# Rotating an 8192 x 8192 matrix by 90 degrees: the last two stores issued in three and four pieces

## The chip, the cores and the metric

The kernel runs on one core of a Trainium2 chip. The metric is the device time of one execution in microseconds (us), the median of several. A core has engines that run side by side (PE multiplies and transposes, DVE and ACT copy, POOL and SP do little here) and 16 DMA engines that move data between the memory (HBM) and the core's on-chip buffer (SBUF), which has 128 partitions. Transfers are issued by SP (here the loads) and by ACT (here the stores); each issuer has its own queue, and both queues are served by the same 16 DMA engines.

## The reference

```python
def setup_inputs():
    return {
        "x": np.random.randn(8192, 8192).astype(np.float32),
        "k": 1,
    }

def reference(x: np.ndarray, k: int) -> np.ndarray:
    return np.rot90(x, k)
```

With k = 1, row i of the output is column 8191 - i of the input: a transpose, and the order of the rows reversed. 268.4 MB are read and 268.4 MB are written; nothing else is computed.

## The kernel before

The input is cut into 16 macro tiles of 1024 rows by 4096 columns. A macro tile is loaded in T = 8 loads of 128 rows (128 partitions of 16 KB, 2 MB each), 128 loads in all. DVE copies each loaded tile into a ring of slots, with the columns reversed (L202). PE transposes blocks of 128 x 128 from the ring into two halves of PSUM (`ps0`, `ps1`, L234). ACT copies each half from PSUM into a store buffer (L265, two copies for each store) and then issues the store (L270), 128 stores of 2 MB in all.

Five buffers of 16 KB for each partition serve all transfers: two for landing loads (`LAND`) and three for stores (`OUTS`); for the first macro tile all five take loads, and for the last eight stores all five take stores. A load waits until DVE has read the buffer's last load; the first copy of a store waits until the last store from its buffer has landed, which is counted in `s_store[b]`, 16 for each transfer.

A store of the first 15 macro tiles writes 512 output rows of 1024 columns. Those of the last macro tile write 1024 output rows of 512 columns (`END` = 4 tiles of rows, two groups of columns): for each of the 128 partitions eight pieces of 2 KB, one in each of eight output rows that lie 128 rows apart. On the SBUF side a partition is one run of 16 KB; `whole_reads` writes it that way into the instruction.

The order of the work is written out by hand, one program for each engine. ACT's program is the loop over the stores: wait for the buffer, copy, copy, wait for both copies (`s_ev`), issue the store, go on to the next. SP's program issues the loads and then, at the end, waits for the last store of every buffer (L188), after which the closing barrier runs. After the last load has landed, only stores remain in the queues; the last eight stores are counted by n = 120 to 127, and the last two of them are n = 126 and n = 127. No later store uses their buffers.

Of the kernel before, what the change touches and what calls it, by code (L numbers as in the profile page):

```python
# [6 lines left out]
P = 128  # L7
# [10 lines left out]
CH = G * P  # L18
# [5 lines left out]
H = 2  # L24
LAND = 2
OUTS = 3


def whole_reads(nc):
# [17 lines left out]
def slot(kk, t, j):  # L47

    at = t * J + j if kk % 2 == 0 else J + t + j * T
    return (at + kk // 2 * (J + 1)) % SLOTS  # L50


def kernel(tc: tile.TileContext, x: bass.AP, k: bass.AP, out: bass.AP):
# [8 lines left out]
    n_out = KK * J  # L62
# [18 lines left out]
    with tc.tile_critical():  # L81
        ident = nc.alloc_sbuf_tensor("ident", [P, P], dt)
        scratch = nc.alloc_sbuf_tensor("scratch", [P, 1], dt)
        bufs = [nc.alloc_sbuf_tensor(f"buf{i}", [P, F], dt) for i in range(LAND + OUTS)]
        ring = nc.alloc_sbuf_tensor("ring", [P, SLOTS * CH], dt)
# [5 lines left out]
        s_id = nc.alloc_semaphore("s_id")  # L91
        s_land = [nc.alloc_semaphore(f"s_land{i}") for i in range(LAND + OUTS)]
        s_store = [nc.alloc_semaphore(f"s_store{i}") for i in range(LAND + OUTS)]
        s_rev = nc.alloc_semaphore("s_rev")
# [4 lines left out]
        def load_buf(m):  # L99
            return m % (LAND + OUTS) if m < T else m % LAND  # L100

        def out_buf(n):
            e = n - (n_out - J)
            if e < 0:
                return LAND + (n + 1) % OUTS
            ends = [load_buf(n_load - 2)]
            ends += [LAND + (n_out - J + i + 1) % OUTS for i in range(OUTS)]
            ends += [load_buf(n_load - 1)]
            return ends[e % len(ends)]
# [25 lines left out]
        def runs(kk, t, lo, hi):  # L135

            at = [slot(kk, t, j) for j in range(lo, hi)]
            i = 0
            while i < len(at):
                n = 1  # L140
                step = at[i + 1] - at[i] if i + 1 < len(at) else 1
                if step > 0:
                    while i + n < len(at) and at[i + n] - at[i + n - 1] == step:
                        n += 1
                else:
                    step = 1
                yield lo + i, n, at[i], step
                i += n

        def load(e, m):  # L150
            r0, c0 = macros[m // T]
            b = load_buf(m)
            e.dma_start(  # L153
                out=bufs[b][:], in_=x[r0 + m % T * P : r0 + (m % T + 1) * P, c0 : c0 + W]
            ).then_inc(s_land[b], 16)

        def uses_before(n_or_m, buf):
            return sum(buf(i) == buf(n_or_m) for i in range(n_or_m))

        for m in range(LAND + OUTS):  # L160
            load(nc.sync, m)
# [1 line left out]
        with nc.Block() as block:  # L163

            @block.gpsimd
            def _(e):
                e.memset(ident[:], 0.0).then_inc(s_id, 1)  # L167
                e.wait_ge(s_id, 1)
                e.affine_select(  # L169
                    out=ident[:],  # L170
                    in_=ident[:],
                    compare_op=mybir.AluOpType.not_equal,
                    fill=1.0,
                    base=0,
                    pattern=[[-1, P]],
                    channel_multiplier=1,
                ).then_inc(s_id, 1)

            @block.sync
            def _(e):  # L180
                for m in range(LAND + OUTS, n_load):
                    last = [i for i in range(m) if load_buf(i) == load_buf(m)]
                    e.wait_ge(s_rev, rev[last[-1], J - 1])
                    load(e, m)
                for b in range(LAND + OUTS):
                    n = sum(out_buf(i) == b for i in range(n_out))
                    if n:
                        e.wait_ge(s_store[b], 16 * n)  # L188

            @block.vector  # L190
            def _(e):
                for m in range(n_load):
                    kk, t = divmod(m, T)
                    b = load_buf(m)
                    a = bufs[b][:].rearrange("p (j c) -> p j c", c=CH)
                    e.wait_ge(s_land[b], 16 * (uses_before(m, load_buf) + 1))
                    for lo, hi, wait in pieces[m]:
                        if wait:
                            e.wait_ge(*wait)
                        for j, n, at, step in runs(kk, t, lo, hi):  # L200
                            v = ring[:, at * CH : (at + (n - 1) * step + 1) * CH]
                            i = e.tensor_copy(  # L202
                                out=bass.AP(
                                    tensor=v.tensor,
                                    offset=v.offset,
                                    ap=[v.ap[0], [step * CH, n], [1, CH]],
                                ),
                                in_=a[:, j : j + n, ::-1],
                            )
                        i.then_inc(s_rev, 1)  # L210

            @block.tensor
            def _(e):
                seen = {}

                def wait(sem, n):
                    if seen.get(sem, 0) < n:
                        seen[sem] = n
                        e.wait_ge(sem, n)

                e.wait_ge(s_id, 2)
                for n, (kk, ts, js) in enumerate(outs):
                    blocks = [(j, g) for j in reversed(js) for g in range(G)]
                    half = len(blocks) // H
                    rows = len(ts) * P

                    def transpose(t, b):
                        j, g = blocks[b]
                        if n:
                            wait(s_ev, H * (n - 1) + b // half + 1)  # L230
                        wait(s_rev, rev[kk * T + t, j])
                        at = slot(kk, t, j) * CH + g * P
                        f = b % half * rows + (t - ts[0]) * P
                        i = e.transpose(  # L234
                            ps[b // half][:, f : f + P], ring[:, at : at + P], ident[:]
                        )
                        if t == ts[-1] and b % half == half - 1:
                            i.then_inc(s_half, 1)
                        elif t == ts[0] and b == len(blocks) - 1:
                            i.then_inc(s_first, 1)  # L240

                    order = [(t, b) for b in range(len(blocks)) for t in ts]
                    if js[0] == 0:
                        order.sort()
                    for t, b in order:
                        transpose(t, b)

            @block.scalar
            def _(e):
                e.wait_ge(s_id, 2)  # L250
                e.copy(scratch[:], ident[:, :1])  # L251
                for n, (kk, ts, js) in enumerate(outs):
                    r0, c0 = macros[kk]
                    rows = len(ts) * P
                    b = out_buf(n)
                    for h in range(H):
                        if h == 0:
                            stores = uses_before(n, out_buf)
                            loads = [i for i in range(n_load) if load_buf(i) == b]
                            if stores:  # L260
                                e.wait_ge(s_store[b], 16 * stores)
                            elif loads:
                                e.wait_ge(s_rev, rev[loads[-1], J - 1])
                        e.wait_ge(s_half, H * n + h + 1)  # L264
                        e.copy(  # L265
                            bufs[b][:, h * F // H : (h + 1) * F // H], ps[h][:]
                        ).then_inc(s_ev, 1)
                    top = M - c0 - (js[-1] + 1) * CH
                    e.wait_ge(s_ev, H * (n + 1))
                    e.dma_start(  # L270
                        out=out[
                            top : top + len(js) * CH, r0 + ts[0] * P : r0 + ts[0] * P + rows
                        ].rearrange("(g m) f -> m g f", m=P),
                        in_=bufs[b][:].rearrange("m (g f) -> m g f", f=rows),
                    ).then_inc(s_store[b], 16)


# [33 lines left out]
```

## Time and profile before

| What | Value |
|---|---|
| time, median of 3 runs | 1266.09 us (1265.68 to 1266.21) |
| time of the profiled execution | 1266.16 us |
| its span, first to last instruction | 1264.2 us |
| PE, DVE, ACT busy | 715.5, 402.9, 467.6 us |
| DMA moved | 537.48 MB, mean 425 GB/s |
| loads (q1), stores (q10) | 268.44 MB each |
| issue of a store on ACT | 0.547 us (median of 128) |
| wait of SP for the last stores (L188) | 63.3 us in two waits |

The time of the profiled execution is 2.0 us longer than its span: that is what lies around the instructions. The page gives busy time by engine and by slice of the span; a DMA share of 1.00 means that all 16 DMA engines are moving a packet. A packet is what one DMA engine moves at a time; the trace lists each with its start, duration, size and queue, but not with the number of its DMA engine. Engine after engine works through its packets with no gap, so a packet's predecessor on the same engine is the one that ends where it starts.

### The profile page before, as it was taken

What the parts mean: (1) busy time and instruction counts of PE and PEld (TensorE: products, weight loads), DVE (VectorE), ACT (ScalarE), POOL (GpSimd) and SP (SyncE); (2) the same over time, 40 slices, a digit from 0 to 9 for tenths busy, and PEclk for the clock granted to TensorE, in tenths of its full rate; (3) what the DMA queues carried; (4) which work ended last, traced back from release to release, by engine and by line L of the source; (5) the groups of instructions that cost most, each with busy time, mean ns of one, the idle gap of its engine ahead of it and who ended that gap; (6) DMA issues with size and microseconds to landing.
All of it is one profiled execution on the core that took longest, in us unless ns stands there. A gap on an engine that the chain in (4) does not pass through costs nothing.

```text
span 1264.2 us, 9359 instructions
## 1 busy us (share of the span) xinstructions
PE 715.5 (57%) x4096; PEld 666.9 (53%) x4096; DVE 402.9 (32%) x313; ACT 467.6 (37%) x258; POOL 0.7 (0%) x6
## 2 busy tenths in 40 slices
PE   1565555665556556665556654565555655546573
PEld 1455555655546555554545544565454654545573
DVE  3322432234322343233342333422234222443210
ACT  0433334333343332433424334243342434324354
POOL 0000000000000000000000000000000000000000
PEclk9976767667777776777777767676676776767777
DMA  9999999999999999999999999999999999999998
GB/s 397 423 429 430 429 427 429 429 430 429 428 429 429 430 430 427 427 430 430 428 430 427 429 430 429 427 427 428 429 428 428 427 430 428 428 427 426 427 425 335
DMA packets 36904, 537.48 MB, mean 425 GB/s; under 512 B 4096, under 2 KB 4096, under 8 KB 4096
## 3 DMA queue, kind: packets, MB, share of 16 engines
q10 hardware_dynamic: 18432, 268.44, 50.0%
q1 hardware_dynamic: 18432, 268.44, 49.8%
q8 instruction: 32, 0.52, 0.2%
q14 instruction: 8, 0.07, 0.0%
HBM read 268.44 MB, written 268.44 MB: 425 GB/s over the span
## 4 chain that ended last, share of the span: by engine, by line
DMA 78%; issue 10%; DVE 5%; ACT 3%; PE 2%; ACTq 0%; SPq 0%
DMA buf<-in_x_dram 77%; DVE ring L202 5%; ACT buf L265 3%; PE ps L234 2%; DMA out_dram<-buf 1%; ACTq L270 0%; SPq L153 0%; ACTq L264 0%; SPq L306 0%; SPq L81 0%
## 5 line engine op out<-in xcount | busy, mean ns | idle before, releaser
L234 PE MATMUL ps<-ident,ring 128*128 128x128 f32 x4096 | 715.5, 353 | 530.3 <-ACT buf L265 394.6
L234 PEld LDWEIGHTS ps<-ident,ring 128*128 128x128 f32 x4096 | 666.9, 188 | 578.7 <-ACT buf L265 433.6
L265 ACT COPY buf<-ps 128x2048 f32<-128x2048 f32 x256 | 466.2, 1870 | 779.6 <-DMA out_dram<-buf 502.0
L202 DVE COPY ring<-buf 128x512 f32<-128x512 f32 (+7 forms) x313 | 402.9, 1336 | 815.4 <-DMA buf<-in_x_dram 814.4
L251 ACT ACT_TABLE_LOAD x1 | 1.3, 1283 | 0.9 <-SPq L81 0.9
L169 POOL TENSOR_SCALAR_AFFINE_SELECT ident<-ident 128x128 f32<-128x128 f32 x1 | 0.3, 292 | 0.2 <-POOL ident L167 0.2
L167 POOL MEMSET ident<- 128x128 f32 x1 | 0.2, 204 | 0.5 <-SPq L81 0.5
L251 ACT COPY scratch<-ident 128x1 f32<-128x1 f32 x1 | 0.2, 191 | 0.0
L292 POOL MEMSET const-bfloat16-1.0<- 128x1 bf16 x1 | 0.1, 102 | 0.0
L292 POOL MEMSET const-uint8-127<- 128x1 uint8 x1 | 0.1, 102 | 0.0
L292 POOL MEMSET const-float32-0.0<- 128x1 f32 x1 | 0.1, 98 | 0.2 <-issue 0.2
L292 POOL MEMSET const-float32-1.0<- 128x1 f32 x1 | 0.1, 98 | 0.0
## 6 DMA issues: line engine op xcount, KB each, us to landing
buf<-in_x_dram SPq DMA_DIRECT2D x128, 2048.0 KB, 16.8
out_dram<-buf ACTq DMA_DIRECT2D x128, 2048.0 KB, 25.6
```

The costliest lines, as they stand in the source:

```text
L167: e.memset(ident[:], 0.0).then_inc(s_id, 1)
L169: e.affine_select(out=ident[:], in_=ident[:], compare_op=mybir.AluOpType.not_equal, fill=1.0, base=0, pattern=[[-1, P]], channel_multiplier=1,
L202: i = e.tensor_copy(out=bass.AP(tensor=v.tensor, offset=v.offset, ap=[v.ap[0], [step * CH, n], [1, CH]],), in_=a[:, j : j + n, ::-1],)
L234: i = e.transpose(ps[b // half][:, f : f + P], ring[:, at : at + P], ident[:])
L251: e.copy(scratch[:], ident[:, :1])
L265: e.copy(bufs[b][:, h * F // H : (h + 1) * F // H], ps[h][:]).then_inc(s_ev, 1)
L292: nc = _bacc.Bacc("TRN2", target_bir_lowering=False, num_devices=1)
```

## The change

The store loop issues the second to last store as three transfers, of partitions 0 to 111, 112 to 119 and 120 to 127, and the last as four, of partitions 0 to 111, 112 to 119, 120 to 123 and 124 to 127. All pieces of a store are issued by ACT one behind the other, after the same wait for both copies, and count into the same semaphore; what waits for it counts pieces instead of stores. The other 126 stores are issued as before, and what is written where is the same.

```diff
+PIECES = {-2: [112, 8, 8], -1: [112, 8, 4, 4]}
...
+        def loads_before(m):
+            return sum(load_buf(i) == load_buf(m) for i in range(m))
+
+        def store_pieces(n):
+            return PIECES.get(n - n_out, [P])
+
+        def stores_of(b, n):
+
+            return sum(len(store_pieces(i)) for i in range(n) if out_buf(i) == b)
...
-                    n = sum(out_buf(i) == b for i in range(n_out))
+                    n = stores_of(b, n_out)
                     if n:
                         e.wait_ge(s_store[b], 16 * n)
...
-                            stores = uses_before(n, out_buf)
+                            stores = stores_of(b, n)
...
-                    e.dma_start(
-                        out=out[
-                            top : top + len(js) * CH, r0 + ts[0] * P : r0 + ts[0] * P + rows
-                        ].rearrange("(g m) f -> m g f", m=P),
-                        in_=bufs[b][:].rearrange("m (g f) -> m g f", f=rows),
-                    ).then_inc(s_store[b], 16)
+                    dst = out[
+                        top : top + len(js) * CH, r0 + ts[0] * P : r0 + ts[0] * P + rows
+                    ].rearrange("(g m) f -> m g f", m=P)
+                    src = bufs[b][:].rearrange("m (g f) -> m g f", f=rows)
+                    p = 0
+                    for k in store_pieces(n):
+                        e.dma_start(out=dst[p : p + k], in_=src[p : p + k]).then_inc(
+                            s_store[b], 16
+                        )
+                        p += k
```

More of the change, by code (lines that the diff above doesn't have):

```diff
@@ L155, in load @@
             ).then_inc(s_land[b], 16)
-        def uses_before(n_or_m, buf):
-            return sum(buf(i) == buf(n_or_m) for i in range(n_or_m))
+        def loads_before(m):
[4 more added lines that the diff above has]
+            return sum(len(store_pieces(i)) for i in range(n) if out_buf(i) == b)
         for m in range(LAND + OUTS):
@@ L195, in _ @@
                     a = bufs[b][:].rearrange("p (j c) -> p j c", c=CH)
-                    e.wait_ge(s_land[b], 16 * (uses_before(m, load_buf) + 1))
+                    e.wait_ge(s_land[b], 16 * (loads_before(m) + 1))
                     for lo, hi, wait in pieces[m]:
```

## The prediction

> **What bounds the kernel now.** I read the page first: the busy share of the DMA engines in 40 slices, then the counts of packets and the queues.
>
> ```profile
> span 1264.2 us, 9359 instructions
> ...
> DMA  9999999999999999999999999999999999999998
> ...
> DMA packets 36904, 537.48 MB, mean 425 GB/s; under 512 B 4096, under 2 KB 4096, under 8 KB 4096
> ...
> q10 hardware_dynamic: 18432, 268.44, 50.0%
> q1 hardware_dynamic: 18432, 268.44, 49.8%
> ```
>
> The reader is to see that the DMA engines are full from the first slice to the last but one, and that no compute engine matters until then. The lines also give the size of the unit of work. The stores (q10) are 128 transfers and 18432 packets, so 144 each: 128 packets of 16 KB, one for each partition, and 16 small ones (the 4096 under 512 B are 16 for each of the 256 transfers), one as the last of each engine. So a store today gives each of the 16 engines 8 packets. The data packets of q10 take 50.0% of 16 x 1264.2 us; over 16384 packets that is 0.617 us each, 26.5 GB/s for an engine.
>
> Then the table of windows over the last 14 us. Its last three columns are granted clock, share of the 16 DMA engines, and GB/s.
>
> ```profile
> 1250.00:1255.00 5.00, 0.00 (x0) 0.00 (x0) 0.00 (x0) 0.00 (x0) 0.00 (x0) 0.50 1.00 419
> 1255.00:1257.00 2.00, 0.00 (x0) 0.00 (x0) 0.00 (x0) 0.00 (x0) 0.00 (x0) 0.50 0.82 344
> 1257.00:1258.00 1.00, 0.00 (x0) 0.00 (x0) 0.00 (x0) 0.00 (x0) 0.00 (x0) 0.50 0.67 279
> 1258.00:1259.00 1.00, 0.00 (x0) 0.00 (x0) 0.00 (x0) 0.00 (x0) 0.00 (x0) 0.50 0.35 147
> 1259.00:1260.00 1.00, 0.00 (x0) 0.00 (x0) 0.00 (x0) 0.00 (x0) 0.00 (x0) 0.50 0.24 98
> 1260.00:1261.00 1.00, 0.00 (x0) 0.00 (x0) 0.00 (x0) 0.00 (x0) 0.00 (x0) 0.50 0.08 33
> 1261.00:1262.00 1.00, 0.00 (x0) 0.00 (x0) 0.00 (x0) 0.00 (x0) 0.00 (x0) 0.50 0.04 16
> 1262.00:1264.20 2.20, 0.00 (x0) 0.00 (x0) 0.00 (x0) 0.00 (x0) 0.00 (x0) 0.50 0.00 0
> ```
>
> Times 16, the share is the number of engines still at work: all up to 1255, about 11 in 1257 to 1258, four in 1259 to 1260, one after 1260. The packet records say it sharper: seven engines send their last small packet at 1256.4 to 1256.5, eight between 1258.5 and 1260.0, and one, which I call the straggler, at 1262.2. It holds the end alone for 2.2 us. Everything behind it (the wait at L188, the closing barrier) takes the 2.0 us to 1264.2.
>
> Last, the timeline of ACT, which issues the stores.
>
> ```profile
> 1239.55 0.55 ACTq L270 DMA_DIRECT2D out_dram<-buf  x1
> ...
> 1243.87 0.55 ACTq L270 DMA_DIRECT2D out_dram<-buf  x1
> 1244.51 3.63 ACT L265 COPY buf<-ps 128x2048 f32<-128x2048 f32 x2 [0.67 <-PE ps L234]
> 1248.17 0.55 ACTq L270 DMA_DIRECT2D out_dram<-buf  x1
> ```
>
> The last two stores are issued at 1243.87 and 1248.17. The early engines finish the store before them at 1246.5 (16 packets of 0.617 ahead of 1256.4) and the second to last at 1251.5, so the queue is always ahead of them.
>
> **The change, part by part.** The edits to the counts of semaphores (L188, the wait before an eviction, the loads' count) add no instruction and no wait on an earlier store, since no other store is cut: 0.
>
> Five more issues on ACT: 0.547 us each. Two of them stand before the copies of the last store, which then begins to issue 2 x 0.59 = 1.2 us later, at 1249.35. At 1235.24 an issue found idle engines and its first packet started at 1236.44, so the data flow 1.2 us after an issue: 1250.55 here. The engines first need them after seven packets of the second to last store, at 1246.5 + 4.3 = 1250.8. So they are hidden, by 0.25 us in the tightest case. If that cover is gone, early engines idle for up to 1.2 us, which matters only if they end last. The last piece is issued by 1251.6, far before it is needed. Slow issues of 0.94 and 1.17 us occur (1222.25, 1226.95); two of these would push early engines by under 1.5 us.
>
> How the packets are dealt out: 112 partitions, dealt like 128, are 7 for each engine. A piece of 8 has eight packets; I take it that they stay whole, one for each of eight engines, always the first eight, and a piece of 4 goes to the first four (bounds: spread evenly over 16, half a packet each; or all on one engine, 4.9 us). The Trainium skill ("DMA: Bandwidth & Descriptors", section "Why a DMA increments its semaphore by 16 and not by 1") deals in the same way, to the lowest-numbered engines; no run here shows it yet. In the two stores together the first four engines then get 14 ordinary packets and 5 from small pieces (19 where they had 16), the next four 14 and 3 (17), the last eight 14.
>
> The price of a packet in a small piece is what the trace doesn't show: eight engines reading eight neighbouring partitions at once. Today each engine has 8 partitions of its own, so 26.5 GB/s may belong to the engine or to a sixteenth of the partitions; both give 425 GB/s. If to the engine, a packet costs 0.617 us, the lower bound. If to the partitions, it depends on which eight share a lane: dealt one by one over the lanes, 0.617 again; eight neighbours on one lane, 8 x 0.617 = 4.9 us, the upper bound; in between, two groups of four, 4 x 0.617 = 2.5 us. I take the middle, 2.5 us: a lane of the partitions' own explains as well as one of the engines why the engines run so evenly at 26.5 GB/s each, and of its three layouts this one lies between. A piece of 4 then also costs 2.5 us. The Trainium skill ("SBUF — State Buffer", section "Door 1: The DMA port swizzle") speaks against the change in just this way: four neighbouring partitions share one of 16 ports, and partitions 0 to 3 alone gave 27.6 GB/s. By its figures a packet of a small piece would be an estimated 2.4 us; by the engine's own row, 0.617.
>
> **The sum.** First four engines: 14 x 0.617 + 5 x 2.5 = 21.1 us where 16 x 0.617 = 9.9 stood: +11.2. Next four: 8.6 + 7.5 = 16.1: +6.2. Last eight: -1.2. The trace has no engine numbers. Seven engines that end within 0.2 us of each other look like neighbours, so I take the first four to be among them: 1256.4 + 11.2 = 1267.6, which is 5.4 later than the straggler's 1262.2. The end behind it is unchanged, so the span is 1269.6. The profiled execution took 1266.16 for a span of 1264.2, 0.07 over the median of 1266.09: **1271.6 us**. If the first four hold ordinary late engines (1260.0), it is 1275.2; if the straggler, 1277.4. With 1.9 us a packet it is 1268.6.
>
> **Rivals.** (A) *The lane belongs to the engine.* A small packet costs 0.617 like any other and only the counts matter. If the straggler is one of the last eight, it sheds two packets: 1262.2 - 1.2 = 1261.0; the early engines have room (1256.4 + 1.9 = 1258.3): **1264.9 us**. If it is of the middle four, +0.6: 1266.8; of the first four, +1.9: 1268.0. For it: no packet of the whole execution shows two engines slowing each other by a factor. Against it: no two engines ever read neighbouring partitions as the small pieces do. The Trainium skill (the DMA page again, "Latency and other measured facts") calls engines 7 and 15 usually slower; by that the straggler is one of them, which leaves 1264.9 and 1266.8. (B) *The cut of 112 itself collides*: seven partitions for each engine no longer match groups of eight, and ordinary packets slow down too. Three of the 14 ordinary packets at double price add 1.9 us to the forecast: 1273.5. For it is the same argument as for the forecast; against, that such collisions are brief. (C) *The pieces are not dealt as I think*: spread evenly over the 16 engines, every engine keeps 16 packets' worth, and the end stays: 1266.2. (D) *A real gain*, over 0.2%: from 1256.45 on, the engines do some 28 engine-us, so a perfect balance would end 4.0 us earlier, at 1262.2 us. But no engine sheds more than two packets here; only a straggler that comes from luck in its last microseconds would allow it.
>
> **How the numbers follow.** 0.2% (2.5 us) is about what a measurement of this kernel can tell from no change. Forecast with its sizes 0.46, own range 1268.7 to 1273; B and the late first four 0.14, 1273 to 1277; together 0.60 slower. A 0.32, of which 1264.9 has 0.22 (its best case has the engines in the order that the straggler needs), 1266.8 and 1268.0 0.10; C 0.03: 0.35 within. D 0.05 faster. The range reaches down to A, as it holds a third, and up into B: 1264.6 to 1273.6; some 0.15 is left out.
>
> **What would show it.** Each step has its sign in the profile of the changed kernel: 133 issues where 128 stood; q10 with 18464 packets (32 more small ones: 160 packets for each cut store) if each piece ends in one small packet for each engine that it uses; in the last 20 us packets of some 2.5 us, and a DMA share of about 0.25 (four engines) for several microseconds at the end. Packets of 0.62 us throughout and a last one near 1261.0 would make A right; an idle stretch between 1250 and 1252 would say that the later issue matters. The prediction is wrong if no packet of the small pieces takes much over 0.62 us.

## The result and the profile after

The changed kernel takes 1271.78 us (median of 4 runs, 1271.16 to 1272.32) against 1265.95 us (1265.68 to 1266.21) for the kernel before: a ratio of 1.0045, with a 95% interval of 1.0034 to 1.0057. It is 5.8 us slower. The profiled execution is the fastest of the four, 1271.16 us for a span of 1269.3 us, 5.1 us longer than before. From the page of the changed kernel:

```profile
span 1269.3 us, 9364 instructions
...
DMA  9999999999999999999999999999999999999997
...
DMA packets 36936, 537.48 MB, mean 423 GB/s; under 512 B 4128, under 2 KB 4128, under 8 KB 4128
...
q10 hardware_dynamic: 18464, 268.44, 50.1%
```

The bytes are the same, and the 32 additional packets are the small ones that close each piece on each engine that it uses: a piece of 8 uses eight engines, a piece of 4 four. Until slice 38 the row of the DMA engines is the same, and no slice's rate differs by more than 4 GB/s. The table of windows over the end of the changed kernel (last three columns: granted clock, share of the 16 DMA engines, GB/s):

```profile
1243.00:1247.00 4.00, 2.42 (x22) 2.14 (x20) 0.00 (x0) 0.40 (x1) 0.00 (x0) 1.00 1.03 414
1247.00:1250.00 3.00, 0.00 (x0) 0.00 (x0) 0.00 (x0) 0.00 (x0) 0.00 (x0) 0.57 1.03 344
1250.00:1253.00 3.00, 0.00 (x0) 0.00 (x0) 0.00 (x0) 0.99 (x1) 0.00 (x0) 0.50 1.00 328
1253.00:1255.00 2.00, 0.00 (x0) 0.00 (x0) 0.00 (x0) 2.00 (x2) 0.00 (x0) 0.50 0.42 131
1255.00:1257.00 2.00, 0.00 (x0) 0.00 (x0) 0.00 (x0) 0.65 (x1) 0.00 (x0) 0.50 0.21 82
1257.00:1262.00 5.00, 0.00 (x0) 0.00 (x0) 0.00 (x0) 0.00 (x0) 0.00 (x0) 0.50 1.01 328
1262.00:1264.00 2.00, 0.00 (x0) 0.00 (x0) 0.00 (x0) 0.00 (x0) 0.00 (x0) 0.50 0.42 156
1264.00:1266.00 2.00, 0.00 (x0) 0.00 (x0) 0.00 (x0) 0.00 (x0) 0.00 (x0) 0.50 0.23 66
1266.00:1267.50 1.50, 0.00 (x0) 0.00 (x0) 0.00 (x0) 0.00 (x0) 0.00 (x0) 0.50 0.05 22
1267.50:1269.30 1.80, 0.00 (x0) 0.00 (x0) 0.00 (x0) 0.00 (x0) 0.00 (x0) 0.50 0.00 0
```

Two things are new. From 1247 to 1253, and again from 1257 to 1262, all engines are busy, yet they move 328 to 344 GB/s where the kernel before, with all engines busy, moved 419: packets last longer. In the packet records, 83 store packets of the changed kernel that start after 1240 take over 0.75 us (the longest 3.1 us); of the kernel before, one does. And between 1253 and 1257 most engines have nothing to do. ACT's part of the chain of waits of the changed kernel (start, length, what) shows why:

```profile
1243.42 0.62 ACTq L285
1244.04 0.04 issue
1244.08 5.16 ACTq L285
1249.23 0.03 issue
1249.26 2.65 ACTq L285
```

The issue of the first small piece holds ACT for 5.16 us and that of the second for 2.65 us, where 0.547 us each was forecast. ACT can only then copy and issue the last store, as its timeline shows:

```profile
1243.42 8.49 ACTq L285 DMA_DIRECT2D out_dram<-buf  x3
1252.01 3.63 ACT L274 COPY buf<-ps 128x2048 f32<-128x2048 f32 x2 [8.62 <-issue]
1255.68 7.25 ACTq L285 DMA_DIRECT2D out_dram<-buf  x4
```

The last store is issued at 1255.68, 7.5 us later than in the profile before. So three explanations compete: slow packets, late issue, and one engine's additional packets.

### The profile page after: what moved, and what is told of

Read it like the earlier page. It is cut to its first block, busy times and chain, and to the rows that moved or that the text cites. A ratio compares the mean times of both kernels' runs of the same rounds, so it can differ in the third digit from the quotient of the medians.

```text
span 1269.3 us, 9364 instructions
## 1 busy us (share of the span) xinstructions
PE 691.0 (54%) x4096; PEld 644.0 (51%) x4096; DVE 402.9 (32%) x313; ACT 467.2 (37%) x258; POOL 0.7 (0%) x6
## 3 DMA queue, kind: packets, MB, share of 16 engines
q10 hardware_dynamic: 18464, 268.44, 50.1%
## 4 chain that ended last, share of the span: by engine, by line
DMA 80%; issue 8%; DVE 5%; ACT 4%; PE 1%; ACTq 1%; SPq 0%
DMA buf<-in_x_dram 67%; DMA out_dram<-buf 12%; DVE ring L211 5%; ACT buf L274 4%; PE ps L243 1%; ACTq L285 1%; SPq L155 0%; ACTq L273 0%; SPq L319 0%; SPq L83 0%
## 5 line engine op out<-in xcount | busy, mean ns | idle before, releaser
L243 PE MATMUL ps<-ident,ring 128*128 128x128 f32 x4096 | 691.0, 345 | 554.4 <-ACT buf L274 426.8
L243 PEld LDWEIGHTS ps<-ident,ring 128*128 128x128 f32 x4096 | 644.0, 184 | 601.2 <-ACT buf L274 465.3
```

Of the source, the lines that this page charges most:

```text
L243: i = e.transpose(ps[b // half][:, f : f + P], ring[:, at : at + P], ident[:])
```

## The experiments

**What a packet of neighbouring partitions costs, by itself.** Behind the end of the kernel before, with nothing else under way, the last buffer is written once more in pieces, each awaited.

```diff
+                for i, which in enumerate(
+                    [(112, 120), (0, 32, 4), (112, 116), (0, 16, 4), (0, 112), (0, 64), (0, 128)]
+                ):
+                    again(*which)
+                    e.wait_ge(s_x, 16 * (i + 1))
+                again(0, 112)
+                again(112, 120)
+                again(120, 128)
```

> The kernel before, and behind its last store, when everything has landed, the last buffer is written again to the same place in pieces, each awaited before the next is issued: partitions 112 to 119 (eight neighbours), every fourth of 0 to 31 (eight), 112 to 115 (four neighbours), every fourth of 0 to 15 (four), 0 to 111, 0 to 63, all 128; then 112, 8 and 8 as in the changed kernel without waits between. The time is not compared; the work behind the end is extra. If 26.5 GB/s belong to the DMA engine, every packet takes 0.61 to 0.63 us in all of them. If they belong to lanes of eight partitions, in two groups of four neighbours, the packets of eight neighbours take 2.4 us (four to a lane), of every fourth partition 0.62, of four neighbours 2.4, of every fourth of 16 0.62, of partitions 0 to 63 about 1.2 (16 engines on eight lanes), of all 128 0.62, and of 112 a mixture. Issue: if a small piece is slow to issue only because the queues are full, its issue takes 0.55 us here; if the issue itself is slow, about 2.6 us for a piece of 8 and 1.3 for one of 4.

The windows of this run, one around the packets of each awaited piece, in that order:

```profile
1263.80:1266.60 2.80, 0.00 (x0) 0.00 (x0) 0.00 (x0) 0.00 (x0) 0.00 (x0) 0.50 0.42 47
1268.10:1268.90 0.80, 0.00 (x0) 0.00 (x0) 0.00 (x0) 0.00 (x0) 0.00 (x0) 0.50 0.39 164
1270.50:1273.20 2.70, 0.00 (x0) 0.00 (x0) 0.00 (x0) 0.00 (x0) 0.00 (x0) 0.50 0.21 24
1274.70:1275.50 0.80, 0.00 (x0) 0.00 (x0) 0.00 (x0) 0.00 (x0) 0.00 (x0) 0.50 0.19 82
1276.90:1283.50 6.60, 0.00 (x0) 0.00 (x0) 0.00 (x0) 0.00 (x0) 0.00 (x0) 0.50 0.79 278
1285.00:1290.40 5.40, 0.00 (x0) 0.00 (x0) 0.00 (x0) 0.00 (x0) 0.00 (x0) 0.50 0.94 194
1291.90:1297.10 5.20, 0.00 (x0) 0.00 (x0) 0.00 (x0) 0.00 (x0) 0.00 (x0) 0.50 0.95 403
```

Share x 16 x length, over the number of packets, is the time of one: eight neighbours 0.42 x 16 x 2.80 / 8 = 2.35 us; every fourth partition of 32, also eight, 0.39 x 16 x 0.80 / 8 = 0.62 us; four neighbours 2.27 us; every fourth of 16, 0.61 us; partitions 0 to 63, 1.27 us; all 128, 0.62 us. The number of partitions and of engines is the same in the first two lines, only the distance between the partitions differs, and the packet costs four times as much. So 26.5 GB/s belong to lanes of partitions: four neighbours share one, and 64 partitions reach half of the lanes. (Partition m always writes the output rows m, m + 128 and so on of its block. The runs therefore don't tell whether the lane lies at the buffer or at the memory; for cutting a store by partitions the two come to the same.) The 112 partitions lie between: a mean of 0.74 us, some packets of 1.5 us, and the last one 6.3 us after the first, where seven packets of 0.62 would take 4.3. The issues of the awaited pieces took 1.25 us (the first) and 0.58 to 0.72 us; without a wait, the last piece of 8 took 1.81 us.

**The cut of 112 with even counts.** Pieces of 112 and 16, so that each engine gets 7 + 1 packets.

```diff
-PIECES = {-2: [112, 8, 8], -1: [112, 8, 4, 4]}
+PIECES = {-2: [112, 16], -1: [112, 16]}
```

> Both stores in pieces of 112 and 16: each of the 16 engines gets 7 + 1 packets, as many as before the change, and no piece leaves engines out. If only the counts mattered, or the slow issue of pieces that use few engines, the time is that of the kernel before: 1266 to 1267. If 112 partitions dealt in sevens collide on the lanes, the straggler still loses 4 to 5 us: 1270 to 1271.5, with packets of over 1 us among the ordinary ones.

1271.32 us (1269.81 to 1272.19), ratio 1.0038 (1.0023 to 1.0052): nearly the whole loss is there without uneven counts and without pieces that leave engines out. The pieces of 16 are neighbours too, and some of their packets are slow (the longest 3.64 us), so the run by itself does not part them from the 112. Its windows show who ends last:

```profile
1257.00:1262.00 5.00, 0.00 (x0) 0.00 (x0) 0.00 (x0) 0.00 (x0) 0.00 (x0) 0.50 1.00 315
1262.00:1264.00 2.00, 0.00 (x0) 0.00 (x0) 0.00 (x0) 0.00 (x0) 0.00 (x0) 0.50 0.10 41
1264.00:1266.00 2.00, 0.00 (x0) 0.00 (x0) 0.00 (x0) 0.00 (x0) 0.00 (x0) 0.50 0.06 25
1266.00:1268.30 2.30, 0.00 (x0) 0.00 (x0) 0.00 (x0) 0.00 (x0) 0.00 (x0) 0.50 0.05 21
```

From 1264 on one engine is left (1/16 = 0.06), for over 4 us, and its packets are 0.62 us again: the straggler, by its place at the end, thrown back by slow packets before. The issue of the piece of 16, which uses all engines, took 7.7 and 1.9 us, so that a slow issue is no property of pieces that use few engines.

**Which lane is hit, and when.** The last store alone is cut in halves, in the two orders. Counts, sizes and issues are the same in both.

```diff
+PIECES = {-1: [(0, 64), (64, 64)]}
```

```diff
+PIECES = {-1: [(64, 64), (0, 64)]}
```

> The last store alone is cut, into partitions 0 to 63 and then 64 to 127; every engine gets 4 + 4 packets, as many as before the change, and no piece leaves engines out. If lanes are shared and the straggler's lane lies in the lower half, the early engines fall upon its lane while it still works there: 2.5 to 3.5 us slower than before, 1268.6 to 1269.6. If only counts or the number of issues mattered: 1265.8 to 1266.4.

> The same two pieces of the last store, the upper half first. Counts, sizes and number of issues are those of the run with the lower half first; only the lanes that are hit early differ. If the straggler's lane lies in the lower half, it is left alone until the second piece: 0.5 to 1.7 us over the kernel before, 1266.6 to 1267.8, and under the run with the lower half first by 1.3 us or more. If the straggler's lane lies in the upper half, the order of the two is the other way round. If lanes play no part, both are equal.

Lower half first: 1268.32 us, ratio 1.0018 (1.0009 to 1.0027), 0.3 us under the expected range. Upper half first: 1266.79 us, 1.0005 (0.9996 to 1.0014). The windows of the two, lower half first on top:

```profile
1260.00:1262.00 2.00, 0.00 (x0) 0.00 (x0) 0.00 (x0) 0.00 (x0) 0.00 (x0) 0.50 0.21 74
1262.00:1264.00 2.00, 0.00 (x0) 0.00 (x0) 0.00 (x0) 0.00 (x0) 0.00 (x0) 0.50 0.06 25
```

```profile
1260.00:1262.00 2.00, 0.00 (x0) 0.00 (x0) 0.00 (x0) 0.00 (x0) 0.00 (x0) 0.50 0.61 172
1262.00:1264.00 2.00, 0.00 (x0) 0.00 (x0) 0.00 (x0) 0.00 (x0) 0.00 (x0) 0.50 0.02 8
```

With the lower half first, the straggler is again left alone after 1262; with the upper half first nearly ten engines work on until 1262, and the last one ends at 1262.96. Upper half first has even more slow packets (74 over 0.75 us against 54), but none on the engine that ends the second to last store last: its packets stay at 0.63 us up to its end at 1262.4. So what counts is not how many packets are slowed, but whose. That the straggler's lane lies in the lower half is inferred from the two orders; the records don't give the partition of a packet.

**The late issue by itself.** Whole stores, and four more copies on ACT before the last store's issue. A first attempt changed nothing, as ACT issued the store without waiting for the copies to end (issued at 1249.57; 1266.20 us, ratio 0.9999, 0.9990 to 1.0008):

```diff
                     e.wait_ge(s_ev, H * (n + 1))
+                    if n == n_out - 1:
+                        for i in range(4):
+                            e.copy(ring[:, i * F // H : (i + 1) * F // H], ps[i % H][:])
```

> The kernel before with whole stores; ACT makes four more copies of 1.87 us (into ring slots that nobody reads any more) ahead of the issue of the last store, so that it comes 7.5 us late, at about 1255.7, as in the changed kernel. If the late issue by itself costs what the change costs, the time rises by 4 to 6 us, to 1270 or more. If it is hidden behind the straggler, which is busy with the second to last store until 1257.2, the early engines idle and catch up: 1265.9 to 1266.8.

The second waits for them (each copy then counts into `s_ev`):

```diff
+                        e.wait_ge(s_ev, H * (n + 1) + 4)
```

> As the run before it with four more ACT copies, which did not delay the issue since ACT issued the store without waiting for them; now ACT waits for their end, so that the whole last store is issued at about 1255.7, as late as in the changed kernel. If the late issue by itself costs what the change costs: 1270 or more. If it is hidden behind the straggler, which is busy with the second to last store until 1257.2: the other engines idle from about 1252 to 1257 and end near 1262, and the time is 1265.9 to 1266.8.

1266.32 us, ratio 0.9999 (0.9990 to 1.0008): no change. Its ACT timeline and its windows:

```profile
1249.00 7.17 ACT L272 COPY ring<-ps 128x2048 f32<-128x2048 f32 x4
1256.20 0.55 ACTq L276 DMA_DIRECT2D out_dram<-buf  x1
```

```profile
1250.00:1252.00 2.00, 0.00 (x0) 0.00 (x0) 0.00 (x0) 2.00 (x2) 0.00 (x0) 0.50 1.00 418
1252.00:1255.00 3.00, 0.00 (x0) 0.00 (x0) 0.00 (x0) 3.00 (x3) 0.00 (x0) 0.50 0.45 186
1255.00:1257.40 2.40, 0.00 (x0) 0.00 (x0) 0.00 (x0) 1.18 (x1) 0.00 (x0) 0.50 0.05 20
1257.40:1262.60 5.20, 0.00 (x0) 0.00 (x0) 0.00 (x0) 0.00 (x0) 0.00 (x0) 0.50 0.95 403
```

Fifteen engines idle for up to 5 us, then all 16 do the last store together and end between 1262.3 and 1262.5, when the straggler would have ended anyway. An issue as late as that of the changed kernel costs nothing.

**The small pieces from another queue.** SP, idle by then, issues them; ACT issues the 112 alone.

```diff
+                    for k in store_pieces(n):
+                        if k < 112:
+                            e.dma_start(out=dst[p : p + k], in_=src[p : p + k]).then_inc(
+                                s_store[b], 16
+                            )
+                        p += k
```

> The small pieces are issued by SP, which is idle by then, so that ACT issues the 112 partitions of the last store right behind its copies, at about 1248.2 instead of 1255.7. If the late issue of the last store is what costs, some 5 us come back: 1266 to 1267. If the straggler's slow packets on shared lanes and its one packet more are what costs, nothing comes back, as it is never idle in the changed kernel: 1271 to 1273.

1273.45 us (1270.8 to 1273.74), ratio 1.0052 (1.0037 to 1.0067), a little above the expected 1271 to 1273. Nothing comes back, though the last 112 partitions are issued at 1246.8. The run isn't clean: that issue itself now takes 3.8 us, and the packets of the two queues mix on the engines.

**Each half of the change alone.**

```diff
+PIECES = {-1: [112, 8, 4, 4]}
```

> Only the last store is cut (112, 8, 4, 4); the second to last is whole. No ACT work stands behind the cut. If the late issue of the last store was the cause, the time falls back to the level of before or below: 1264.9 to 1266.5. If collisions on the lanes are, the straggler meets them while the early engines work on the last 112 partitions: 1269.5 to 1271.5.

```diff
+PIECES = {-2: [112, 8, 8]}
```

> Only the second to last store is cut (112, 8, 8); the last is whole, but issued late because ACT is held by the small pieces. If collisions on the straggler's lane cost most: 1269 to 1273, with the straggler last by itself again. If the late issue of the last store is what costs in this half of the change, the last store's packets of all engines end together, and there is an idle stretch of 2 us or more on the straggler too.

> The changed kernel once more, on the same chip as the three others of this group, for comparison with them: 1270.5 to 1272.5.

Only the last: 1268.97 us, ratio 1.0023 (1.0014 to 1.0033), 2.9 us, somewhat under what was expected of collisions and far over the other theory. Only the second to last: 1270.70 us, 1.0033 (1.0021 to 1.0045), 4.6 us; the straggler ends last (1268.0 in its trace), and no stretch of 2 us in which it idles was found. The changed kernel again, on the same chip as the latter: 1272.06 us, 1.0046 (1.0034 to 1.0059), 5.9 us. The halves' losses add up to 7.5 us, more than the whole.

**Two whole stores issued one behind the other**, the second to last held back until the last is copied:

```diff
+                    held.append((n, b, top, r0, ts, js, rows))
+                    if n == n_out - 2:
+                        continue
+                    for n, b, top, r0, ts, js, rows in held:
```

> Whole stores, but the second to last is held back and issued together with the last, one right behind the other, at about 1248.2. If an issue takes long because it follows closely upon another one with stores still in the queue, the second takes over 1 us; if it takes long because of the cut, both take 0.55 us. The time should stay within 0.5 us of the kernel before, as the straggler has work until 1252.2 without them.

The issues took 0.547 and 0.621 us, and the time is 1266.09 us, ratio 1.0000 (0.9991 to 1.0009). Following closely upon another issue is not enough to make one slow. Nor is a cut piece (0.58 to 0.72 us when the queue is empty, but for the first one), nor the use of few engines (the piece of 16). The longest issues, up to 7.7 us, are of transfers behind, or beside, a cut store that is not yet done. But whole stores are slow to issue at times too, ahead of any cut, as two lines of the changed kernel's ACT timeline show:

```profile
1220.90 1.85 ACTq L285 DMA_DIRECT2D out_dram<-buf  x1
1226.51 1.15 ACTq L285 DMA_DIRECT2D out_dram<-buf  x1
```

By the packet records, the whole stores that took 0.94 to 1.96 us found 155 to 186 packets of earlier stores still to be moved, although others that found as many were quick. The second whole store of this run found only 151, and the small piece at 1244.08 in the changed kernel 225, so this run does not rule out that the amount in the queue plays a part. It is not all: the other small pieces of the changed kernel found 47 to 120 and took 1.26 to 3.63 us. What the issues wait for was not settled.

## Why the prediction was right, and where it was not

The predicted 1271.6 us lies 0.2 us from the median, and the mechanism that it rested on is shown: the rate belongs to lanes of partitions, and moving partitions to other engines makes engines share lanes. But the sum behind the number is not the way in which the time was lost: it let the first four engines end last, at 1267.6, and another engine ended last, at 1267.3. That the two lie so near each other is luck.

- *The price of a packet in a small piece*, taken as 2.5 us between bounds of 0.617 and 4.9: 2.35 and 2.27 us, measured by itself. The term was sized rightly. The Trainium skill ("SBUF — State Buffer", section "Door 1: The DMA port swizzle") has 27.6 GB/s for partitions 0 to 3 and 196 GB/s for 0 to 63; here four neighbours took 65.5 KB in 2.57 us, 25.5 GB/s, and the lower half 1.05 MB in 5.26 us, 199 GB/s. The trace agrees.
- *Five such packets on each of the first four engines* set the end in the prediction. In the changed kernel the price was not paid in that form at the end: since the small pieces of the last store are issued 3.7 and 1.7 us apart, its packets don't meet all at once, and those after 1262.1 last 0.61 to 1.57 us. The first four engines end at 1266.3 or before, not at 1267.6. The other engines' small packets of the second to last store, of up to 3.1 us, are over by 1256.3, before most engines begin the last store at 1256.96; the wait for its late issue hid them.
- *The engine that ends last* is still the straggler, at 1267.3, 5.1 us later than before. The packet records give its account. It finishes the store ahead of the two cut ones, a whole store, at 1254.6 instead of 1252.2 (+2.4), with packets of up to 2.21 us while the early engines are at the 112 partitions of the next. Then it does 17 packets where it had 16 (+0.6). Four of these, of 0.72, 0.80, 0.81 and 2.47 us, cost 2.4 us over 0.611; the others are 0.611 instead of 0.626 (-0.2). Its three packets of small pieces took 0.61 us each, so none of the slow ones is among those. That is rival B's mechanism, the collisions of the 112 partitions dealt in sevens, which the prediction held for brief (0.14 for it and the late first four) and priced at three packets. The run with 112 and 16 loses nearly as much with even counts. That the slow packets meet others on the straggler's lane is inferred from the price and from the two orders. This is the step that was mis-sized: the collisions were looked for among the small pieces and on the engines that get them, and they are worst on the engine that was late already.
- *The straggler's place.* It closes five pieces in the two stores (three and two), so it is one of the four engines that take part in the pieces of 8 but not in those of 4, and its lane lies in the lower half by the two orders. The Trainium skill ("DMA: Bandwidth & Descriptors", section "Latency and other measured facts") calls engines 7 and 15 usually slower, but puts that down, as a guess, to transfers issued by GpSimd, which issues none here; 7 would fit both, but no run here names the engine.
- *The issues* were forecast at 0.547 us each and hidden by 0.25 us. They took 1.3 to 5.2 us for the small pieces, the last store came 7.5 us late, and most engines idled. That step was wrong in size, but an issue just as late costs nothing with whole stores, because the straggler has work until 1257.
- *Rival A*, lanes of the engines' own, is refuted by every fourth partition against neighbours. *Rival C*, pieces spread over all engines, is refuted by the count of small packets: 18464 in q10, as forecast. *Rival D* did not come.

None of the versions tried beats the kernel before. Upper half first, the second to last store held back and the last store issued late are within what can be told from it. There is a reason for this in the lanes: the straggler's partitions have to pass its lane whichever engine moves them, and a lane passes one packet per 0.6 us, hardly more than the straggler by itself manages. Giving its packets to engines that idle therefore can't end the store earlier; this last step is argued from the prices, and no run tried it alone.

## What to carry to other kernels

Before work is shifted from a late DMA engine to early ones, ask what the rate belongs to: here to lanes of partitions, so that a piece of few neighbouring partitions, or a count that is not dealt like the full 128, slows the very engine that was to be relieved. Measure the price by itself behind the end of the kernel, with neighbouring and with spaced partitions; it takes one run. And idle engines near the end are no loss as long as one engine sets the end: 15 engines idled for up to 5 us at no cost.

## What was not expected of the hardware

- The issue of a transfer behind a cut store took up to 6.9 us of ACT's time for 8 partitions (with only the second to last store cut; 5.2 us in the changed kernel) and 7.7 us for 16, against 0.547 us for most whole stores.
- ACT issues a store without waiting for its own copies ahead of it to end, unless a semaphore says so: in the first attempt the issue was recorded at 1249.57, 0.01 us after the start of the first of four copies.
- All 16 engines started together on a whole store end within 0.2 us of each other (1262.3 to 1262.5), so the ragged end of the kernel before is a lag gathered earlier, and not a slowness of the straggler in the last store: there its eight packets take 5.0 us, as those of the other late engines do.
